# A trunk of convolution, attention and expert layers on one Trainium2 core: the convolution's first chunk, the softmax scaling and the layernorm affine go to other engines, and the layernorm starts two gate tiles sooner

## The chip, the cores and the metric

The kernel runs on one core of one Trainium2 chip. Its engines are TensorE (PE in the profile), VectorE (DVE), ScalarE (ACT), GpSimd (POOL) and SyncE (SP, which here only issues transfers). Each engine runs its own instructions in the order written and waits on semaphores for the others. The metric is the device time of one execution in microseconds (us), as the median of several runs.

## The reference, cut to what matters

The model has two layers (`DEPTH = 2`) over 272 tokens (16 meta tokens and 256 of the input) of width 1024. A layer is a mixer block followed by a block of experts ("peer"). The mixer block projects the normed tokens once and splits the result:

```python
z = h @ w_in
conv_in, c_q, c_kv, k_rope, gate_logits = split(z)
u = conv_in[..., :512] * sigmoid(conv_in[..., 512:])
u = causal_depthwise_conv(u, conv_w, conv_b)           # 31 taps, 512 channels
u = silu(layernorm(u, conv_ln_g, conv_ln_b))           # (u - mu) * rsqrt(var + eps) * g + b
y_conv = u @ w_conv_out
o = chunk_causal_attention(q, k, v)                    # 8 heads, softmax over the keys
y_mla = o @ w_mla_out
merged = sigmoid(gate_logits[..., :1024]) * y_conv + sigmoid(gate_logits[..., 1024:]) * y_mla
x = x + merged @ w_out
```

The expert block scores 16,384 experts per token, picks 16 for each of 8 heads and adds up their outputs. It takes most of the time and is untouched by the change.

## The kernel before, in words

Everything is kept transposed: features on the 128 partitions, tokens along the free dimension. `T` is 272; in the last layer the 16 meta tokens are not needed further on, so the work after the projections runs on `TQ` = 256 columns (`t0` = 16). The schedule is manual: each engine's order is the order in which the Python code emits instructions. Generators (`attention`, `conv2`, `layernorm`) are advanced by `next(...)` between matmul tiles, so that small work of DVE, ACT and POOL falls beside PE's tiles. Weights stream through a ring of four 1 MB buffers (`wraw`), two tiles each, issued by SP.

The part of a layer that the change touches goes so:

- Eight projection tiles for the four chunks of `u` (`ztile`, 8 matmul calls each, two PE instructions a call); DVE and ACT form `u` in `upad`, chunk by chunk.
- **The gate loop**, `for i in range(16)` at line 772: each round is one projection tile on PE (`z`), DVE multiplies it by the token scale into `gt` (line 774), and then `next(att)` and `taps(...)` are called twice. `att` has two steps a round: one puts scores, transposes or the mix with `v` on PE, the other puts the softmax (line 461), its scaling (`scale`, line 478) or copies on ACT and DVE.
- **The convolution** runs meanwhile. Chunks 1 to 3 are 93 taps on DVE (`conv`, line 624), dealt out by the table `TAPS`. Chunk 0 is `conv2`: ACT multiplies the shifted input by a tap's weight (line 631), POOL adds it to `acc` (line 632), tap by tap.
- **The layernorm** (line 679) may begin when all taps are done: PE sums over features (`st`), DVE subtracts the mean, ACT squares, PE sums again (`st2`), DVE makes the reciprocal root in three Newton steps (`rsqrt_steps`, lines 173 to 178), multiplies (702), applies gain and bias (704), ACT takes the sigmoid (706), DVE multiplies by it (710), ACT and DVE split the result into two reduced-precision halves (711, 713) for `uu`.
- **The eight half tiles.** `half_tile(0..3)` multiply the attention output `oo` by `w_mla_out`, `half_tile(4..7)` the convolution's `uu` by `w_conv_out`. Each is 24 matmuls into two PSUM tiles from a pool `z` of three. The weights come as a high half (`high(i)`, ACT, line 653) and a low half (`low(i)`, DVE, line 658). `high(i)` and `low(i)` write buffers that rotate over three places (`wuq`; `seln` and `upad`; `kh` or `acc` and `sqa`). DVE then multiplies the gate in (811) for the first four, or merges (829 to 834) for the last four.
- Eight tiles with `w_out` follow, then the expert block.

`gates(n)` (line 769) lets ACT take the sigmoid of gate tiles in place, two a round, and the rest after the loop. `high(0)`/`low(0)` come in round 14, `high(1)`/`low(1)` after the loop. So before the change the order around the loop's end is set by these lines:

```python
        if i == 14:
            high(0, 1)
            low(0)
    gates(16)
    run_all(att)
    ...
    high(1, 1)
    low(1)
```

## Time and profile before

| What | Value |
|---|---|
| Median of 3 runs (lowest to highest) | 1739.38 us (1739.05 to 1741.44) |
| Profiled execution, its own time | 1741.49 us |
| Its span, first to last instruction | 1739.7 us |
| PE busy, DVE busy, ACT busy, POOL busy | 1706.7, 1157.5, 521.6, 327.1 us |
| Gate loop of the first layer (62 to 147 us): PE, DVE busy | 85.0, 76.5 of 85.0 us |
| End of layernorm and half tiles, first layer (147.0 to 184.1 us): PE, DVE busy | 32.2, 31.5 of 37.1 us |
| The same in the second layer (1023.0 to 1058.85 us): PE busy | 31.0 of 35.85 us |
| POOL's additions for chunk 0, both layers | 60, 51.2 us |
| DVE's taps for chunks 1 to 3, both layers | 180 at lines 624, 90.6 us |

A busy time is the sum of an engine's instruction times; matmuls overlap in the array, so a busy PE says only that it had work. "Idle before" is the gap ahead of an instruction, with the event that ended it. The chain of waits is followed back from the last instruction and shows what set the end.

### The profile page before, as it was taken

The numbers are of one execution on the slowest core, as the hardware profiler recorded it, in microseconds if no ns is written. First come the engines' busy times: TensorE is split into PE (matmuls) and PEld (weight loads), VectorE is DVE, ScalarE is ACT, GpSimd is POOL, SyncE is SP. The second block draws the span as 40 slices with busy tenths as digits, with TensorE's granted clock in tenths as the row PEclk, the third lists the DMA queues.
The fourth block names the chain that finished last, engine by engine and source line by source line (L and its number), as shares of the span: only waits on it lengthen the run. The fifth ranks groups of instructions, "written<-read, shape, count | busy, mean of one in ns | idle before, by whom it ended". The sixth has DMA issues, their size and how long they took to land.

```text
span 1739.7 us, 30197 instructions
## 1 busy us (share of the span) xinstructions
PE 1706.7 (98%) x11867; PEld 1605.3 (92%) x11867; DVE 1157.5 (67%) x2977; ACT 521.6 (30%) x1536; POOL 327.1 (19%) x392
## 2 busy tenths in 40 slices
PE   9999999999999999999999999999999999999998
PEld 7677989989999999999986889899999999999998
DVE  6698678897888544444456987797878885333332
ACT  3444413335544110000024445133355441000000
POOL 0130012222112222322201310112221113122220
PEclk9999999999999999999999999999999999999999
DMA  6223556999999999999962245579999999999995
GB/s 237 98 97 122 194 194 263 372 375 422 420 420 420 421 420 415 421 420 420 418 242 97 98 146 191 197 298 367 396 422 424 423 417 418 393 384 387 400 384 210
DMA packets 80814, 559.42 MB, mean 322 GB/s; under 512 B 9240, under 2 KB 12248, under 8 KB 13208
## 3 DMA queue, kind: packets, MB, share of 16 engines
q1 hardware_dynamic: 49488, 338.54, 49.2%
q0 software_dynamic: 30464, 218.35, 30.9%
q8 instruction: 93, 1.52, 0.3%
q10 hardware_dynamic: 720, 0.60, 0.1%
q14 instruction: 49, 0.40, 0.1%
HBM read 556.18 MB, written 1.05 MB: 320 GB/s over the span
## 4 chain that ended last, share of the span: by engine, by line
PE 65%; DMA 11%; DVE 10%; issue 9%; POOL 3%; ACT 2%; SPq 0%; POOLq 0%; DVEq 0%; ACTq 0%
PE po L56 27%; PE z L56 19%; PE A L56 13%; DMA wraw<-vn 6%; DMA gb<-uv,iww 5%; PE aps L56 3%; POOL gb L1287 2%; DVE va L1298 1%; DVE gb L1312 1%; PE wp L56 1%; PE sc L56 1%; PE xp L56 0%; DVE ex L1011 0%; DVE wuq L658 0%; DVE ex L1008 0%
## 5 line engine op out<-in xcount | busy, mean ns | idle before, releaser
L56 PE MATMUL A<-xh,wraw 128*128 128x160 f32 x3776 | 535.2, 301 | 1.2 <-ACT idxT L925 1.2
L1312 DVE SCALAR_TENSOR_TENSOR gb<-gb,xr 128x1024 f32<-128x1024 f32 x208 | 254.3, 1223 | 406.4 <-DMA gb<-uv,iww 406.0
L56 PEld LDWEIGHTS A<-xh,wraw 128*128 128x128 f32 x3776 | 518.3, 191 | 1.6 <-issue 1.6
L56 PE MATMUL z<-xg,wraw 128*128 128x272 f32 (+2 forms) x1408 | 328.0, 390 | 0.6 <-DMA wraw<-w_in 0.6
L1287 POOL DMA_INDIRECT gb<-uv,iww x208 | 221.6, 1065 | 538.8 <-DVE va L1298 376.2
L56 PEld LDWEIGHTS z<-xg,wraw 128*128 128x128 f32 (+1 forms) x1408 | 258.4, 189 | 54.6 <-issue 8.7
L56 PE MATMUL po<-Xh,wraw 128*128 128x160 f32 x2080 | 287.4, 300 | 3.5 <-DMA wraw<-vn 2.8
L56 PEld LDWEIGHTS po<-Xh,wraw 128*128 128x128 f32 x2080 | 283.2, 190 | 6.6 <-DMA wraw<-vn 5.3
L56 PE MATMUL po<-X,wraw 128*128 128x160 f32 x2016 | 278.4, 301 | 5.3 <-DMA wraw<-vn 2.8
L56 PEld LDWEIGHTS po<-X,wraw 128*128 128x128 f32 x2016 | 275.9, 191 | 7.4 <-DMA wraw<-vn 4.3
L1298 DVE SCALAR_TENSOR_TENSOR va<-gb,am,va 128x1024 f32<-128x1024 f32 x203 | 259.6, 1279 | 1.5 <-ACT am L1323 1.3
L1322 ACT ACTIVATE am<-am 128x1 f32<-128x1 f32 x208 | 41.3, 198 | 595.7 <-DVE gb L1312 595.7
L1226 ACT ACTIVATE ohA<-ohE,wlo 128x128 f16<-128x128 f16 x320 | 105.2, 428 | 6.2 <-DVE ohE L1223 5.5
L632 POOL TENSOR_TENSOR acc<-acc,cp 128x272 f32<-128x272 f32 (+1 forms) x60 | 51.2, 853 | 232.1 <-ACT cp L631 222.8
L1286 POOL COPY warm<-wraw 1x1 f32<-1x1 f32 x86 | 32.8, 382 | 325.1 <-DMA wraw<-vn 324.9
L624 DVE SCALAR_TENSOR_TENSOR acc<-upad,cols,acc 128x272 f32<-128x272 f32 (+1 forms) x180 | 90.6, 556 | 0.2
L1323 ACT ACTIVATE am<-am,iww 128x1 f32<-128x1 f32 x208 | 61.3, 295 | 6.8
L1237 ACT ACTIVATE Xh<-wp 128x260 f32<-128x260 f32 (+18 forms) x80 | 25.0, 313 | 125.1 <-DVE Xh L1234 113.6
L1223 DVE TENSOR_TENSOR ohE<-ioh,idxT 128x512 f16<-128x512 f16 x160 | 60.2, 417 | 0.0
L56 PE MATMUL wp<-ohE,ohA 128*128 128x128 f16 x640 | 51.4, 219 | 0.7 <-DVE ohA L1224 0.7
L56 PEld LDWEIGHTS <-ohA 128*128 128x128 f16 x640 | 43.2, 97 | 5.9 <-DVE ohA L1224 1.3
L56 PE MATMUL A<-xh,we 128*128 128x160 f32 x320 | 45.3, 299 | 0.0
(355 smaller groups left out, 1571.7 us busy)
## 6 DMA issues: line engine op xcount, KB each, us to landing
wraw<-vn SPq DMA_DIRECT2D x128, 1024.0 KB, 10.6
wraw<-u SPq DMA_DIRECT2D x118, 1024.0 KB, 10.1
wraw<-w_in SPq DMA_DIRECT2D x27, 1024.0 KB, 4.8
wraw<-wq SPq DMA_DIRECT2D x16, 1024.0 KB, 4.8
we<-u SPq DMA_DIRECT2D x10, 1024.0 KB, 7.1
wraw<-w_out SPq DMA_DIRECT2D x8, 1024.0 KB, 4.7
wraw<-w_mla SPq DMA_DIRECT2D x4, 1024.0 KB, 4.7
wraw<-w_conv SPq DMA_DIRECT2D x4, 1024.0 KB, 5.1
```

Of the source, the lines that this page charges most:

```text
L56: PE.matmul(o, l, r, start=start, stop=stop, skip_group_check=True)
L624: V.scalar_tensor_tensor(acc[:, c, t0:], u_, weight(c, k), acc[:, c, t0:], op0=OP.mult, op1=OP.add)
L632: G.tensor_tensor(acc[:, 0, t0:], acc[:, 0, t0:], u_[:, t0:], op=OP.add)
L1223: V.tensor_tensor(E[q], ioh[:, None].to_broadcast(full), pairs(q, b), op=OP.is_equal)
L1226: S.activation(A_[1][:, t // 2, :, t % 2], E[0][:, t // 2, :, t % 2], AF.Copy, scale=wlo[:, 4 * b + t:4 * b + t + 1])
L1237: S.activation(x_, p[:, :, a:b].rearrange("p t j -> p j t"), AF.Copy, scale=1.0 / WS)
L1286: G.tensor_copy(warm[0:1], state["w"][0:1, 0:1])
L1287: G.indirect_dma_start(out=g_, out_offset=None, in_=a[f"uv{l}"], in_offset=bass.IndirectOffsetOnAxis(ap=iww[i].bitcast(I32)[:, m // 16, 0, ...
L1298: V.scalar_tensor_tensor(vac[i], r, m_, vac[i], op0=OP.mult, op1=OP.add)
L1312: V.scalar_tensor_tensor(u_, u_, 1.0, xrs[i], op0=OP.mult, op1=OP.mult, accum_out=m_)
L1322: S.activation(m_, m_, AF.Gelu_apprx_tanh)
L1323: S.activation(m_, m_, AF.Copy, scale=iww[i][:, m // 16, 1, m % 16:m % 16 + 1])
```

## The change

Five edits, all in the mixer block of both layers:

1. Chunk 0 of the convolution: ACT makes products of three taps in a tile of three slices (`cp`, two buffers; the first three go to `part`), and one accumulating transfer issued by POOL adds the three slices to `part` inside SBUF. Ten such transfers a layer; the POOL additions are gone. At the end DVE adds the three slices of `part` in two operations. `taps` advances `conv2` three times a round where it was twice.
2. `TAPS` deals the DVE taps out sooner, so that the layernorm is created in round 11, not 13, and its first steps stand in rounds 12 to 15.
3. The softmax scaling (line 484) goes from DVE to ACT.
4. The layernorm's gain and bias go from DVE to ACT: the sigmoid takes them as its scale and bias, and a second activation writes the affine result in place.
5. In `half_tile` the second PSUM tile comes from the pool `aps` (five buffers), not `z`; in the loop over the first four half tiles the layernorm's steps come ahead of `high` and of the gate products.

```diff
--- before.py
+++ after.py
@@ -24,7 +24,7 @@
 EPS = 1e-6
 NEG = -3.0e38
 WS = 16384.0
-TAPS = [2, 2, 5, 5, 6, 6, 6] + [8] * 9
+TAPS = [3, 3, 6, 6] + [8] * 12
 SCALE = 96 ** -0.5
 NC_ = 58
 GROUPS = ((64, 32), (64, 32))
@@ -481,7 +481,7 @@
                 for i in range(2):
                     for e in range(2):
                         x = 2 * i + e
-                        V.tensor_scalar(pr[i][:, e], pr[i][:, e], sm[:, x:x + 1], None, op0=OP.mult)
+                        S.activation(pr[i][:, e], pr[i][:, e], AF.Copy, scale=sm[:, x:x + 1])
 
             def turn(p):
 
@@ -623,14 +623,24 @@
                 else:
                     V.scalar_tensor_tensor(acc[:, c, t0:], u_, weight(c, k), acc[:, c, t0:], op0=OP.mult, op1=OP.add)
 
+        part = mp.tile([128, 3, T], F32, name="part")
+
         def conv2():
 
-            S.activation(acc[:, 0, t0:], upad[:, 0, t0:T], AF.Identity, scale=weight(0, 0), bias=bias(0))
-            for k in range(1, KW):
-                u_ = mp.tile([128, T], F32, name="cp", bufs=4)
-                S.activation(u_[:, t0:], upad[:, 0, k + t0:k + T], AF.Copy, scale=weight(0, k))
-                G.tensor_tensor(acc[:, 0, t0:], acc[:, 0, t0:], u_[:, t0:], op=OP.add)
+            for k in range(0, KW, 3):
+                u_ = mp.tile([128, 3, T], F32, name="cp", bufs=2) if k else part
+                n = min(3, KW - k)
+                for x in range(n):
+                    S.activation(u_[:, x, t0:], upad[:, 0, k + x + t0:k + x + T], AF.Copy if k + x else AF.Identity,
+                                 scale=weight(0, k + x), bias=0.0 if k + x else bias(0))
+                    yield
+                if k:
+                    G.dma_start(part[:, 0:n, t0:], u_[:, 0:n, t0:], accum_op=OP.add)
+            for _ in range(4):
                 yield
+            V.tensor_add(acc[:, 0, t0:], part[:, 0, t0:], part[:, 1, t0:])
+            V.tensor_add(acc[:, 0, t0:], acc[:, 0, t0:], part[:, 2, t0:])
+            yield
 
         parts = {}
 
@@ -671,7 +681,7 @@
             next_w()
             ps = []
             for f in range(2):
-                p = zp.tile([128, 512], F32, name="z", bufs=3)[:, :TQ]
+                p = (aps() if f else zp.tile([128, 512], F32, name="z", bufs=3))[:, :TQ]
                 three(i, p, (src[:, 0], src[:, 1]), 4 * f, range(4), 0, 3)
                 ps.append(p)
             return ps
@@ -701,9 +711,9 @@
             for c in range(4):
                 V.tensor_mul(acc[:, c, t0:], acc[:, c, t0:], rl)
             for c in range(4):
-                V.tensor_scalar(acc[:, c, t0:], acc[:, c, t0:], cl[:, C_LG + c:C_LG + c + 1],
-                                cl[:, C_LB + c:C_LB + c + 1], op0=OP.mult, op1=OP.add)
-                S.activation(sg[:, c, :TQ], acc[:, c, t0:], AF.Sigmoid)
+                g_, b_ = cl[:, C_LG + c:C_LG + c + 1], cl[:, C_LB + c:C_LB + c + 1]
+                S.activation(sg[:, c, :TQ], acc[:, c, t0:], AF.Sigmoid, scale=g_, bias=b_)
+                S.activation(acc[:, c, t0:], acc[:, c, t0:], AF.Identity, scale=g_, bias=b_)
             yield
             yield
             for c in range(4):
@@ -773,16 +783,17 @@
             z = ztile(t0)
             V.tensor_mul(gt[i // 8][:, i % 8, t0:], z, rs[:, t0:])
             if ln is None:
-                more = next(att, "end")
-                taps(TAPS[i] // 2, 1)
+                next(att, None)
+                taps(TAPS[i] // 2, 2)
                 next(att, None)
                 taps(TAPS[i] - TAPS[i] // 2, 1)
-                if more == "end" and min(ck.values()) == KW and next(cvp, "end") == "end":
-                    run_all(cvp)
+                if min(ck.values()) == KW and next(cvp, "end") == "end":
                     ln = layernorm()
             else:
                 next(ln, None)
+                next(att, None)
                 next(ln, None)
+                next(att, None)
             if "exp" in vt:
                 gates(min(i + 1, ng[0] + 2))
             if i == 14:
@@ -805,14 +816,14 @@
         low(1)
         for i in range(4):
             ps = half_tile(i, oo)
+            next(ln, None)
+            next(ln, None)
             if i < 3:
                 high(i + 2, 1)
             for f in range(2):
                 V.tensor_mul(gt[1][:, 2 * i + f, t0:], gt[1][:, 2 * i + f, t0:], ps[f])
             if i < 3:
                 low(i + 2)
-            next(ln, None)
-            next(ln, None)
         run_all(ln)
         high(5, 1)
         low(5)
```

What this does to the order at the loop's end, first layer. ACT from the square of the layernorm on (`wuq`, `seln` and `kh` are the high halves of half tiles 0, 1 and 2, `g_607` and `g_596` the second eight gate tiles, `sqa` the sigmoid's result), before:

```order
L769 ACTIVATE g_607<-g_607 128x272 x2
L653 ACTIVATE wuq<-wraw 128x1024
L769 ACTIVATE g_607<-g_607 128x272 x6
L653 ACTIVATE seln<-wraw 128x1024
L653 ACTIVATE kh<-wraw 128x1024
L653 ACTIVATE wuq<-wraw 128x1024
L706 ACTIVATE sqa<-acc 128x272 x4
L653 ACTIVATE seln<-wraw 128x1024
L711 ACTIVATE uk<-acc 128x272 x4
```

and after, up to the first of four pairs of lines 715 and 716 (one pair a chunk):

```order
L699 ACTIVATE sqa<-acc 128x272 x4
L779 ACTIVATE g_595<-g_595 128x272 x4
L779 ACTIVATE g_596<-g_596 128x272 x2
L663 ACTIVATE wuq<-wraw 128x1024
L715 ACTIVATE sqa<-acc,cols_61 128x272
L716 ACTIVATE acc<-acc,cols_61 128x272
```

The first layernorm square (699) and these pairs have moved ahead of most of the gate sigmoids. Still on ACT, behind the fourth pair:

```order
L779 ACTIVATE g_596<-g_596 128x272 x6
L663 ACTIVATE seln<-wraw 128x1024
L721 ACTIVATE uk<-acc 128x272 x4
L663 ACTIVATE kh<-wraw 128x1024
L663 ACTIVATE wuq<-wraw 128x1024
```

The layernorm's activations, which stood behind four high halves, now stand ahead of `seln` (half tile 1), and the six last gate sigmoids with them.

DVE at the same place (`wuq`, `upad`, `kh` are the low halves of half tiles 0, 1, 2; the operation on `z` at line 774 or 784 is the gate product of a projection tile), before:

```order
L658 TENSOR_TENSOR wuq<-wraw,wuq 128x1024
L774 TENSOR_TENSOR g_607<-z,rq_ym 128x272
L695 TENSOR_SCALAR rq_x<-aps 128x272
L173 TENSOR_SCALAR rq_w<-rq_x 128x272
L174 TENSOR_SCALAR rq_yl<-rq_w 128x272
L176 SCALAR_TENSOR_TENSOR rq_w<-rq_yl 128x272
L177 TENSOR_TENSOR rq_w<-rq_w,rq_x 128x272
L178 SCALAR_TENSOR_TENSOR rq_yl<-rq_w,rq_yl 128x272
L658 TENSOR_TENSOR upad<-wraw,seln 128x1024
L811 TENSOR_TENSOR g_607<-g_607,z 128x272 x2
L658 TENSOR_TENSOR kh<-wraw,kh 128x1024
```

and after:

```order
L178 SCALAR_TENSOR_TENSOR rq_yl<-rq_w,rq_yl 128x272
L668 TENSOR_TENSOR wuq<-wraw,wuq 128x1024
L784 TENSOR_TENSOR g_596<-z,rq_ym 128x272
L712 TENSOR_TENSOR acc<-acc,rq_yl 128x272 x4
L668 TENSOR_TENSOR upad<-wraw,seln 128x1024
L720 TENSOR_TENSOR acc<-acc,sqa 128x272 x4
L723 TENSOR_TENSOR uk<-acc,uk 128x272 x4
L824 TENSOR_TENSOR g_596<-g_596,z 128x272
L824 TENSOR_TENSOR g_596<-g_596,aps 128x272
L668 TENSOR_TENSOR kh<-wraw,kh 128x1024
```

All three Newton steps and the product with the root now stand ahead of half tile 1's low half, and the rest of the layernorm stands between the low halves of half tiles 1 and 2.

## The prediction

> **What bounds the kernel now.** I read the page's busy times first, then stretches around the mixer block's stages, then the chain of waits, and last each engine in order of time.
>
> ```profile
> PE 1706.7 (98%) x11867; PEld 1605.3 (92%) x11867; DVE 1157.5 (67%) x2977; ACT 521.6 (30%) x1536; POOL 327.1 (19%) x392
> ```
>
> ```profile
> 62.00:147.00 85.00, 85.00 (x463) 66.63 (x462) 76.52 (x191) 33.49 (x92) 24.73 (x28) 1.00 0.31 110
> 147.00:184.10 37.10, 32.18 (x212) 28.89 (x211) 31.49 (x66) 18.84 (x34) 0.00 (x0) 1.00 0.40 147
> 1023.00:1058.85 35.85, 31.00 (x211) 28.67 (x210) 0.95 0.41 150
> ```
>
> PE has work for 98% of the span: a change can win only where PE stands idle. In a stretch's row stand its length, then the busy time of PE, its weight load, DVE, ACT and POOL, then PE's granted clock (the row of the second layer has PE and weight load alone). Through the gate loop (62 to 147 us) PE is never idle, though DVE is busy for 76.5 of 85 us. **So whatever only makes DVE's load lighter in the loop (no scaling, no POOL beside it) is worth nothing by itself.** PE's idle time within reach is 37.10 - 32.18 = 4.9 us in the first layer and 35.85 - 31.00 = 4.85 in the second, around the half tiles. The chain of waits has a piece there (start, length, engine, tile) that shows the pattern, a high half on ACT, a low half on DVE; then PE in order of time:
>
> ```profile
> 167.65 1.05 ACT seln L653
> 168.70 0.02 issue
> 168.72 1.23 DVE upad L658
> ```
>
> ```profile
> 135.73 11.27 PE L56 MATMUL z<-xg,wraw 128*128 128x272 f32 x48
> 146.83 2.00 PE L56 MATMUL aps<-acc,ones 128*128 128x272 f32 x8
> 148.67 3.83 PE L56 MATMUL z<-xg,wraw 128*128 128x272 f32 x16
> 152.33 2.00 PE L56 MATMUL aps<-sqa,ones 128*128 128x272 f32 x8
> 153.97 3.47 PE L56 MATMUL z<-sq,wuq 128*128 128x272 f32 x24
> 157.27 0.29 PE L56 MATMUL z<-sq,seln 128*128 128x272 f32 x1
> 158.21 0.40 PE L56 MATMUL z<-sq,upad 128*128 128x272 f32 x1 [0.65 <-DVE upad L658]
> 161.21 1.68 PE L56 MATMUL z<-sq,kh 128*128 128x272 f32 x12
> 185.71 0.29 PE L56 MATMUL z<-xh,acc 128*128 128x272 f32 x1
> ```
>
> Half tile 0 starts at 153.97, the work behind half tile 7 at 185.71: 31.7 us. One half tile takes 157.27 - 153.97 = 3.30, or, its first matmul apart, 161.21 - 158.21 = 3.00 for 23, so 3.13 for 24. Eight would take 25.0 to 26.4: the stage loses 5.3 to 6.7 us.
>
> **The change, part by part.** From 135.73 on PE has four projection tiles and the layernorm's two sums before half tile 0, in both kernels; only the order among them changes. With PE never idle before, half tile 0 can start at 153.97 again. Three tiles take 146.83 - 135.73 = 11.1, one 3.7. Round 15's tile is now the last thing ahead of 153.97, so round 14's is ready at 153.97 - 3.7 = 150.3.
>
> *DVE.* The second Newton step is queued behind the gate product of round 14, which waits for that tile.
>
> ```profile
> 159.90 0.43 DVE L176 SCALAR_TENSOR_TENSOR rq_w<-rq_yl 128x272 f32<-128x272 f32 x1
> 162.63 0.78 DVE L811 TENSOR_TENSOR g<-g,z 128x272 f32<-128x272 f32 x2
> 163.33 1.22 DVE L658 TENSOR_TENSOR wuq<-wraw,wuq 128x1024 fp32r<-128x1024 f32 x1
> 164.46 1.49 DVE L702 TENSOR_TENSOR acc<-acc,rq_yl 128x272 f32<-128x272 f32 x4
> 176.17 0.43 DVE L829 TENSOR_TENSOR az<-g,z 128x272 f32<-128x272 f32 x1
> 179.89 0.43 DVE L829 TENSOR_TENSOR az<-g,z 128x272 f32<-128x272 f32 x1
> ```
>
> A gate product takes 0.35 (two in 163.33 - 162.63), two Newton steps 162.63 - 159.90 = 2.73, a low half 1.13 until the next may start (164.46 - 163.33) and 1.22 until its result. So: 150.3 + 0.35 + 2.73 = 153.4 low half 0 starts, ready at 154.6; round 15's gate product and the first product with the root (0.43) end at 153.4 + 1.13 + 0.35 + 0.43 = 155.3. Half tile 0 waits 0.6 us for its low half and ends at 154.6 + 3.0 = 157.6.
>
> *ACT* then has eight activations with scale and bias per partition, the in-place one of each pair waiting for its partner, then six gate sigmoids, and only then the high half of half tile 1 (`seln`).
>
> ```profile
> 152.87 2.17 ACT L769 ACTIVATE g<-g 128x272 f32<-128x272 f32 x6
> 154.94 1.05 ACT L653 ACTIVATE seln<-wraw 128x1024 fp32r<-128x1024 f32 x1
> 192.21 0.51 ACT L186 ACTIVATE xg<-hT,cols 128x272 f32<-128x272 f32 x1
> 192.62 0.41 ACT L190 ACTIVATE sq<-hT 128x272 f32<-128x272 f32 x1
> 703.22 0.20 ACT L1322 ACTIVATE am<-am 128x1 f32<-128x1 f32 x1 [4.43 <-DVE gb L1312]
> 703.45 0.29 ACT L1323 ACTIVATE am<-am,iww 128x1 f32<-128x1 f32 x1
> ```
>
> A scaled activation of this shape takes 0.51 and lets the next start after 0.41 (192.62 - 192.21); one that waits for the activation ahead of it starts 0.03 after that one's end (703.45 against 703.42). A pair is 0.51 + 0.03 + 0.41 = 0.95. The trace has no sigmoid with scale and bias. Plain ones come every 0.35 (six in 2.07), so a pair is at least 0.70; with both waiting it is at most 1.08. I take 0.95, from the row with the nearest operands. Four pairs 3.8, six sigmoids 154.94 - 152.87 = 2.07, `seln` 1.05, low half 1 on DVE 1.22: 155.3 + 8.1 = 163.5 with the hand-overs (0.02 each). **Half tile 1 has both halves at 163.5, and PE is free from 157.6: it waits 5.9 us in one piece.** Before, half tile 1 ran from 158.2.
>
> Behind that low half DVE has the product with the sigmoid (4 x 0.35), the split (4 x 0.35), the gate products of half tile 0 (0.7) and low half 2 (1.22): 163.5 + 4.7 = 168.2 for half tile 2. From there the layernorm is through. DVE has two gate products and a low half for each half tile (0.7 + 1.13), later a merge and a low half (179.89 - 176.17 = 3.7, three times, against PE's 3.1 to 3.3, entered more than a tile ahead), and ACT a high half and two copies. PE runs on: 168.2 + 6 x 3.13 (or 3.30) - 0.1 = 186.9 to 187.9, against 185.71: 1.2 to 2.2 us later. **I take 1.6.**
>
> The second layer has the same order at 256 columns.
>
> ```profile
> 1029.27 3.45 PE L56 MATMUL z<-sq,wuq 128*128 128x256 f32 x24
> 1053.79 3.10 PE L56 MATMUL z<-uk,wuq 128*128 128x256 f32 x24
> 1056.73 0.28 PE L56 MATMUL z<-uk,seln 128*128 128x256 f32 x1
> 1060.38 0.28 PE L56 MATMUL z<-xh,acc 128*128 128x256 f32 x1
> ```
>
> In the first layer half tile 2 starts 168.2 - 153.97 = 14.2 behind half tile 0; with operations 256/272 as long on the way I take 14.0. A clean half tile is 1056.73 - 1053.79 = 2.94: 1029.27 + 14.0 + 6 x 2.94 - 0.1 = 1060.8, against 1060.38: **0.4 later** (with 3.3 a half tile 2.6).
>
> *PE's clock.* The second layer's gaps already cost clock before the change:
>
> ```profile
> 1042.00:1046.00 4.00, 1.80 (x13) 1.59 (x14) 3.23 (x9) 2.37 (x6) 0.00 (x0) 1.00 0.43 182
> 1046.90:1050.40 3.50, 3.50 (x18) 3.50 (x19) 3.04 (x7) 2.00 (x2) 0.00 (x0) 0.52 0.00 0
> ```
>
> PE was busy for 1.8 of 4 us, and the next 3.5 us ran at a granted clock of 0.52. That loss is inside the 1060.38 above. The gap of 5.9 us should do the same, now in both layers: half tile 1 takes about 4.7 instead of 3.0 us, from 163.5 to 168.2, when half tile 2 gets its low half at the earliest. So most of it is hidden: I charge **0.3 a layer**. If the low clock outlasts half tile 1, it costs up to 1.7 a layer (3.5 us at half).
>
> The Trainium skill (TensorE: Matmul & The Clock Gate, Part 1: The HAM clock gate) says that the array falls to half clock after an idle window of about 3.4 us and returns after a busy one, and that the windows run free of the work. The 0.52 for 3.5 us agrees; the fall after a stretch that was busy 1.8 of 4 us does not need a wholly idle window. By that rule alone the old gaps would have cost nothing and the new one a window's half, 1.7 a layer, 1744.8.
>
> *Taps and transfers* lie beside PE's tiles.
>
> ```profile
> 69.99 2.54 DVE L624 SCALAR_TENSOR_TENSOR acc<-upad,cols,acc 128x272 f32<-128x272 f32 x6
> 131.00 4.42 DVE L624 SCALAR_TENSOR_TENSOR acc<-upad,cols,acc 128x272 f32<-128x272 f32 x8
> 119.82 3.83 PE L56 MATMUL z<-xg,wraw 128*128 128x272 f32 x16
> 130.49 3.93 PE L56 MATMUL z<-xg,wraw 128*128 128x272 f32 x16
> ```
>
> ```profile
> wraw<-w_in SPq DMA_DIRECT2D x27, 1024.0 KB, 4.8
> mv<-svm POOLq DMA_DIRECT2D x4, 4.0 KB, 3.8
> ```
>
> Eight taps beside POOL's additions take 4.42; without, 2.54 x 8/6 = 3.4. Two rounds of the loop are 130.49 - 119.82 = 10.7 on PE, one 5.3; DVE's new round is 3.4 + 0.35 and about 1 us of attention. So eight taps a round fit, and the last one ends before the first sum is due at 135.73 + 3.7 = 139.4. An accumulating transfer is 128 x 3 x 272 x 4 bytes = 408 KB. A plain one lands in 3.8 (4 KB from POOL) to 4.8 us (1 MB); that the destination is read as well could double it, 9.6. Each waits for the one before and one is due a round, so they pile up from 5.3 us on. I take 4.5, nearest the plain rows: no cost. ACT gets some 7 us of scaling a layer into 85 - 33.5 = 51.5 us of idle time, and the softmax's scaled rows are wanted two rounds later. The second PSUM pool only removes waits that the sums above no longer hold.
>
> **Sum.** 1.6 + 0.4 + 2 x 0.3 = 2.6 us on the profiled execution's span of 1739.7 (its own time is 1741.49, near the top of the runs shown). I set the sum on the median: 1739.4 + 2.6 = 1742.0.
>
> **Rivals.** (a) *The clock stays low past half tile 1*: 1.7 instead of 0.3 a layer, or two such windows: 1745 to 1748. For it: the fall after shorter gaps. Against it: that fall lasted 3.5 us, hardly more than the half tile it would hit.
>
> (b) *The layernorm's move pays.* If half tile 1 is not held up, the stage loses only the 0.6, not 5.3 to 6.7, and the second layer keeps its clock: 5 us a layer, 1729. Every us off the gap is one a layer; below a gap of about 2.9 the time passes under 1735.9. Against it: ACT works in order, and the 8.1 us between 155.3 and 163.5 are rows; the lowest pair (0.70) brings 1 us a layer, 1740.
>
> (c) *The accumulating transfers are late.* DVE then stands at its first addition of `part` at the end of round 9, with the gate products and soon PE's tiles behind it. At 7 us each the ten end 10 x (7 - 5.3) = 17 us late; DVE's slack from there to 139.4 is about 14 us of PE's rounds less 7 of its own work. So PE loses some 10 a layer, 1760. Against it: the plain rows; for it: no row of an accumulating one. The Trainium skill (SBUF — State Buffer, Who interferes with whom) says that DVE can keep POOL off a shared port and so delay its descriptors; the slow taps beside POOL show that the two share something, no run here shows a late descriptor.
>
> **Chances.** The forecast 0.55, with its own range 1739 to 1744; (a) 0.22; (b) 0.13; (c) 0.10. A measurement of this kernel tells a change of 0.2%, 3.5 us, from none: 1735.9 to 1742.9. Slower: (c) 0.10, most of (a) 0.18, the forecast's upper end 0.08, in all 0.36. Faster: (b) 0.12. Same: 0.52. The range leaves out (b)'s 1729 and (c): 1738 to 1749.
>
> **What would show it.** Right: PE idle 5 to 6 us ahead of half tile 1's first matmul on `upad`, released by line 668; about 0.6 ahead of half tile 0's second; next to none from half tile 2 on; a granted clock near 0.5 for some 3.5 us behind the gap; taps at 0.42; transfers landing in under 5 us. Wrong: a gap under 3 us there (b); gaps in the gate loop or DVE waiting at line 641 (c); a low clock in half tile 2 (a).

## The result: 0.8% slower, and the profile after

| | Before | After |
|---|---|---|
| Median of the runs timed together (5 each) | 1740.43 us | 1753.88 us (1751.76 to 1759.54) |
| Ratio, 95% interval | | 1.0078 [1.0061, 1.0095] |
| Profiled execution: its time, its span | 1741.49, 1739.7 us | 1754.29, 1752.5 us |

The forecast was 1742.0 us with a range of 1738 to 1749. The kernel came out 13.4 us slower than before, 5 us above the range.

The first rows are the page's busy times of the changed kernel; the second fence has three stretches of it (length, then busy PE, weight load, DVE, ACT, POOL, granted clock, DMA share, GB/s): the first layer's gate loop, its half tiles, and a piece of the second layer's gate loop.

```profile
PE 1712.1 (98%) x11867; PEld 1607.8 (92%) x11867; DVE 1126.6 (64%) x2941; ACT 541.1 (31%) x1576; POOL 320.1 (18%) x352
```

```profile
62.00:147.00 85.00, 85.00 (x464) 66.60 (x462) 64.47 (x184) 43.61 (x116) 8.89 (x10) 1.00 0.56 149
147.00:184.10 37.10, 30.53 (x199) 28.43 (x198) 26.51 (x54) 17.67 (x30) 0.00 (x0) 0.91 0.41 144
975.00:1000.00 25.00, 22.23 (x106) 17.82 (x105) 15.15 (x43) 14.98 (x44) 5.02 (x4) 0.86 0.67 142
```

The third of these stretches in the kernel before:

```profile
975.00:1000.00 25.00, 25.00 (x144) 20.46 (x142) 24.59 (x62) 14.63 (x45) 8.19 (x11) 1.00 0.24 85
```

In the first layer DVE is 12 us lighter in the gate loop and PE as full as before, which brings nothing; the half tiles have lost 1.65 us of PE's busy time and part of its clock. Both were forecast. The second layer's gate loop was not: PE, never idle there before, stands for 2.8 of 25 us, and the mean granted clock of the stretch is 0.86. Cutting the two profiled executions at the same places tells what each stage took (us; "to half tile 0" runs from the layer's first projection tile, in the first layer from the span's start; "half tiles" from the first matmul of half tile 0 to the first behind half tile 7):

| Stage | Before | After | Difference |
|---|---|---|---|
| Layer 1, to half tile 0 | 153.97 | 153.44 | -0.5 |
| Layer 1, half tiles | 31.74 | 33.61 | +1.9 |
| Layer 2, to half tile 0 | 140.45 | 146.34 | **+5.9** |
| Layer 2, half tiles | 31.11 | 33.40 | +2.3 |
| All else (eight tiles with `w_out`, expert blocks, the end) | 1382.4 | 1385.7 | +3.3 |

The last row is mostly the expert blocks, in which no edit lies. Over the fourteen kernels of this text the first layer's block took 673.6 to 678.1 us between the same two places (675.2 before, 676.5 after), in no order that follows an edit. So of these 3.3 us I explain nothing and take them as scatter.

**First layer, half tiles.** PE in order of time (start, length, idle time ahead and what ended it), and ACT:

```profile
153.44 0.49 PE L56 MATMUL z<-sq,wuq 128*128 128x272 f32 x1
154.63 1.66 PE L56 MATMUL z<-sq,wuq 128*128 128x272 f32 x11 [0.69 <-DVE wuq L668]
163.00 0.59 PE L56 MATMUL z<-sq,seln 128*128 128x272 f32 x1 [5.21 <-ACT seln L663]
164.26 0.59 PE L56 MATMUL z<-sq,upad 128*128 128x272 f32 x1 [0.67 <-DVE upad L668]
168.69 1.88 PE L56 MATMUL z<-sq,kh 128*128 128x272 f32 x12
187.05 0.29 PE L56 MATMUL z<-xh,acc 128*128 128x272 f32 x1
```

```profile
155.36 0.62 ACT L715 ACTIVATE sqa<-acc,cols 128x272 f32<-128x272 f32 x1 [9.04 <-DVE acc L712]
156.01 0.62 ACT L716 ACTIVATE acc<-acc,cols 128x272 f32<-128x272 f32 x1
156.53 0.60 ACT L715 ACTIVATE sqa<-acc,cols 128x272 f32<-128x272 f32 x1
160.00 2.01 ACT L779 ACTIVATE g<-g 128x272 f32<-128x272 f32 x6
161.91 1.04 ACT L663 ACTIVATE seln<-wraw 128x1024 fp32r<-128x1024 f32 x1
```

The picture is the forecast one: a single gap ahead of half tile 1 (5.21 us for its high half, 0.67 more for its low half), the pairs and six gates ahead of `seln` on ACT, no gap from half tile 2 on, and the work behind half tile 7 at 187.05 against a forecast of 186.9 to 187.9. Only the pairs are longer than forecast: four take 160.00 - 155.36 = 4.64, one 1.16.

**Second layer, gate loop.** PE, ACT and POOL of the changed kernel (POOL with two rows of the first layer ahead):

```profile
978.25 3.62 PE L56 MATMUL z<-xg,wraw 128*128 128x256 f32 x16
981.71 1.60 PE L56 MATMUL aps<-kh,xh 98*128 98x144 f32 x8
986.08 2.04 PE L56 MATMUL aps<-t,vt 128*64 128x256 f32 x12 [2.77 <-ACT t L504]
988.05 6.41 PE L56 MATMUL z<-xg,wraw 128*128 128x256 f32 x16
```

```profile
979.35 0.91 ACT L634 ACTIVATE cp<-upad,cols 128x256 f32<-128x256 f32 x2 [4.11 <-DMA part<-cp]
984.64 0.91 ACT L634 ACTIVATE cp<-upad,cols 128x256 f32<-128x256 f32 x2 [1.96 <-DMA part<-cp]
985.45 0.57 ACT L504 ACTIVATE t<-aps 128x512 f32<-128x512 f32 x1
```

```profile
86.47 0.86 POOL L638 DMA_DIRECT2D part<-cp  x1 [7.11 <-ACT cp L634]
90.99 0.86 POOL L638 DMA_DIRECT2D part<-cp  x1 [3.66 <-DMA part<-cp]
...
957.31 1.41 POOL L638 DMA_DIRECT2D part<-cp  x1 [87.05 <-ACT cp L634]
962.54 1.29 POOL L638 DMA_DIRECT2D part<-cp  x1 [3.82 <-DMA part<-cp]
972.95 1.26 POOL L638 DMA_DIRECT2D part<-cp  x1 [9.12 <-DMA part<-cp]
979.80 1.25 POOL L638 DMA_DIRECT2D part<-cp  x1 [5.59 <-DMA part<-cp]
985.09 1.25 POOL L638 DMA_DIRECT2D part<-cp  x1 [4.04 <-DMA part<-cp]
...
1012.62 0.90 POOL L638 DMA_DIRECT2D part<-cp  x1 [3.99 <-DMA part<-cp]
```

Read from below. POOL issues a transfer when the one ahead has landed. In the first layer that takes 4.5 us here (90.99 - 86.47; 4.5 to 5.1 where one waits for the one ahead, once 6.4); in the second these rows are 5.2, 10.4, 6.9 and 5.3 us apart, and over all ten the mean is (1012.62 - 957.31) / 9 = 6.15 us. ACT wants to write products into one of two buffers, has to stand until a transfer has freed it (4.11, then 1.96 us), and only behind that come the copies `t` at 985.45. PE, which mixes with `t`, stands 2.77 us, and its next projection tile takes 6.41 us instead of 3.62, at a granted clock of 0.58 (988.0 to 994.5 us). The gap and the slow tile together are 5.6 of the stage's 5.9 us.

### The profile page after: what moved, and what is told of

It reads as the page before. It is cut to its first block, busy times and chain, and to the rows that moved or that the text cites. A ratio compares the mean times of both kernels' runs of the same rounds, so it can differ in the third digit from the quotient of the medians.

```text
span 1752.5 us, 30137 instructions
## 1 busy us (share of the span) xinstructions
PE 1712.1 (98%) x11867; PEld 1607.8 (92%) x11867; DVE 1126.6 (64%) x2941; ACT 541.1 (31%) x1576; POOL 320.1 (18%) x352
## 3 DMA queue, kind: packets, MB, share of 16 engines
q0 software_dynamic: 35648, 225.92, 33.4%
## 4 chain that ended last, share of the span: by engine, by line
PE 64%; DMA 15%; issue 8%; DVE 8%; ACT 2%; POOL 2%; POOLq 0%; SPq 0%; DVEq 0%; ACTq 0%
PE po L56 24%; PE z L56 18%; PE A L56 15%; DMA wraw<-vn 8%; DMA gb<-uv,iww 5%; PE aps L56 4%; POOL gb L1298 2%; DMA part<-cp 1%; PE wp L56 1%; DVE gb L1323 1%; DVE va L1309 1%; PE sc L56 1%; DMA wraw<-u 1%; PE xp L56 0%; DVE upad L668 0%
## 5 line engine op out<-in xcount | busy, mean ns | idle before, releaser
L1298 POOL DMA_INDIRECT gb<-uv,iww x208 | 233.7, 1124 | 521.0 <-DVE va L1309 375.3
L1297 POOL COPY warm<-wraw 1x1 f32<-1x1 f32 x86 | 43.8, 509 | 317.7 <-DMA wraw<-vn 317.6
L624 DVE SCALAR_TENSOR_TENSOR acc<-upad,cols,acc 128x272 f32<-128x272 f32 (+1 forms) x180 | 76.8, 486 | 0.2
L638 POOL DMA_DIRECT2D part<-cp x20 | 21.3, 1065 | 246.3 <-ACT cp L634 176.1
L1103 POOL TENSOR_TENSOR xh<-xg,rq_ym 128x272 f32<-128x272 f32 (+1 forms) x16 | 11.3, 739 | 199.9 <-DVE sv L906 102.4
```

The source lines that it names most:

```text
L624: V.scalar_tensor_tensor(acc[:, c, t0:], u_, weight(c, k), acc[:, c, t0:], op0=OP.mult, op1=OP.add)
L638: G.dma_start(part[:, 0:n, t0:], u_[:, 0:n, t0:], accum_op=OP.add)
L1297: G.tensor_copy(warm[0:1], state["w"][0:1, 0:1])
L1298: G.indirect_dma_start(out=g_, out_offset=None, in_=a[f"uv{l}"], in_offset=bass.IndirectOffsetOnAxis(ap=iww[i].bitcast(I32)[:, m // 16, 0, ...
```

## The experiments

Two causes are to be told apart and sized: the transfers in the second layer, and ACT's queue ahead of half tile 1. Each kernel is the changed one with the edit shown, unless another is named. The kernel before was timed beside each; its median was 1741.2 to 1741.7 us in the three groups of experiments. The half tiles' length is given as layer 1 / layer 2.

| Kernel | Median, us | Ratio to before, 95% | Layer 2 to half tile 0 | Half tiles |
|---|---|---|---|---|
| before | 1740.43 | 1 | 140.45 | 31.74 / 31.11 |
| after | 1753.88 | 1.0078 [1.0061, 1.0095] | 146.34 | 33.61 / 33.40 |
| taps side by side | 1745.67 | 1.0020 [1.0011, 1.0029] | 140.20 | 33.59 / 32.35 |
| side by side, three buffers | 1745.09 | 1.0019 [1.0010, 1.0028] | 140.18 | 33.83 / 33.03 |
| plain transfers | 1745.53 | 1.0025 [1.0016, 1.0035] | 140.18 | 33.59 / 32.32 |
| three buffers, sums in three runs as in the change | 1763.18 | 1.0123 [1.0104, 1.0142] | 155.53 | 34.74 / 33.43 |
| additions on GpSimd | 1748.59 | 1.0035 [1.0022, 1.0047] | 140.19 | 33.59 / 32.97 |
| half tile 1 sooner | 1752.87 | 1.0059 [1.0047, 1.0072] | 146.08 | 33.57 / 31.36 |
| side by side, softmax scaling on DVE | 1744.51 | 1.0017 [1.0008, 1.0026] | 140.18 | 33.57 / 32.31 |
| side by side, affine on DVE | 1742.52 | 1.0007 [0.9998, 1.0017] | 140.18 | 32.56 / 30.48 |
| side by side, halves sooner, gates spread | 1739.68 | 0.9993 [0.9984, 1.0002] | 140.18 | 30.63 / 29.33 |
| the same, affine on DVE | **1731.64** | **0.9946 [0.9933, 0.9960]** | 140.17 | 27.17 / 26.15 |
| the same, additions on GpSimd | 1736.31 | 0.9977 [0.9962, 0.9992] | 140.21 | 27.07 / 27.34 |
| before, in that order | 1742.02 | 1.0005 [0.9996, 1.0014] | 140.42 | 31.73 / 31.13 |

### The taps side by side

In the second layer the three slices of a group are 272 columns long, of which 256 are moved: three runs of 1024 bytes a partition. This kernel packs them into one of 3072.

```diff
-        part = mp.tile([128, 3, T], F32, name="part")
+        def three_taps(name, bufs=1):
+            t_ = mp.tile([128, 3 * T], F32, name=name, bufs=bufs)
+            return t_[:, 0:3 * TQ].rearrange("p (x t) -> p x t", x=3)
+        part = three_taps("part")
...
-                u_ = mp.tile([128, 3, T], F32, name="cp", bufs=2) if k else part
+                u_ = three_taps("cp", 2) if k else part
```

> The changed kernel with the three taps side by side alone: one run of 3072 bytes a partition in the second layer, two buffers as in the change. If the three runs a partition make the second layer's transfers slow (4.8 to 6.4 us, one of 10, against 4.5 us for one run in the first layer), they fall to about 4.5 us, ScalarE's waits at line 634 shrink to under 1 us each and 3 to 6 us come back: 1748 to 1751 us. If it is the weights' traffic beside them that makes them slow, the waits stay and the time is 1753 to 1755 us.

It took 1745.67 us, 8.2 below the change and lower than I had expected. POOL again:

```profile
969.65 0.85 POOL L642 DMA_DIRECT2D part<-cp  x1 [6.99 <-ACT cp L638]
974.09 0.86 POOL L642 DMA_DIRECT2D part<-cp  x1 [3.58 <-DMA part<-cp]
979.31 0.85 POOL L642 DMA_DIRECT2D part<-cp  x1 [4.37 <-DMA part<-cp]
```

Where one waits for the one ahead, transfers now start 4.4 to 5.2 us apart (5.31 in the mean over all ten), an issue takes 0.86 instead of 1.26, some issues wait for ACT's products and not for a landing, and the stage up to half tile 0 is back at 140.20: the gap in PE's gate loop is gone, though ACT still stands up to 3.5 us at a group. The same bytes in one run instead of three are worth the whole 5.9 us. The second layer's half tiles are 1 us shorter as well, but that does not follow the transfers: over the seven kernels with the same code there they take 32.3 to 33.4 us.

### A third buffer, with and without the packing

The first edit is on top of the taps side by side:

```diff
-            t_ = mp.tile([128, 3 * T], F32, name=name, bufs=bufs)
-            return t_[:, 0:3 * TQ].rearrange("p (x t) -> p x t", x=3)
+            t_ = mp.tile([128, 3 * TQ], F32, name=name, bufs=bufs)
+            return t_.rearrange("p (x t) -> p x t", x=3)
...
-                u_ = three_taps("cp", 2) if k else part
+                u_ = three_taps("cp", 3 if t0 else 2) if k else part
```

> The changed kernel, with two edits to the accumulating transfers: the three taps lie side by side (in the second layer one run of 3072 bytes a partition instead of three of 1024), and in the second layer there are three buffers of products instead of two. Theory W (ScalarE, in order, stands at the first tap of a group until the transfer of two groups back has landed, and TensorE then misses the copies t that stand behind it): with a third buffer a transfer has two rounds of some 3.7 us; the waits of ScalarE at line 634 in the second layer (3.87, 2.78, 4.11, 1.96 us) go, TensorE's busy time between the gate tiles is unbroken again, the stage up to st is some 6 us shorter, and the kernel takes 1747 to 1749 us. Rival S (the softmax scaling that was put on ScalarE makes the copies t late): no change, 1752 to 1755. Rival Q (the transfers' queue itself is too slow, over 5 us each whatever the buffers): the wait stays at the last groups and moves to VectorE's addition of the parts; 1750 to 1753.

1745.09 us, below all three expectations: packing and a third buffer together gain no more than packing alone, so with the packing done a third buffer adds nothing. So I gave the change three buffers and left its sums in three runs (the products lie side by side here):

```diff
-                u_ = mp.tile([128, 3, T], F32, name="cp", bufs=2) if k else part
+                u_ = part[:, :, t0:] if not k else mp.tile([128, 3, TQ], F32, name="cp", bufs=3 if t0 else 2)
...
-                    G.dma_start(part[:, 0:n, t0:], u_[:, 0:n, t0:], accum_op=OP.add)
+                    G.dma_start(part[:, 0:n, t0:], u_[:, 0:n], accum_op=OP.add)
```

> The changed kernel with three buffers of products in the second layer, and the sums still in three runs of 1024 bytes a partition. In the profile of the change a transfer is issued only when the one ahead has landed, 5.1 to 6.9 us apart (10.4 once), so a third buffer lends one transfer of slack but no pace. If the buffers were the cause: 1745 to 1747 us. If the pace of the transfers is: ScalarE's waits come one group later and the time is 1748 to 1753 us.

1763.18 us, outside both expectations: worse than two buffers by 9 us. VectorE shows why:

```profile
1012.42 1.66 DVE L624 SCALAR_TENSOR_TENSOR acc<-upad,cols,acc 128x256 f32<-128x256 f32 x4
1025.19 0.43 DVE L641 TENSOR_TENSOR acc<-part 128x256 f32<-128x256 f32 x1 [11.11 <-DMA part<-cp]
```

With a third buffer the transfers are no faster (6.72 us apart in the mean, 6.15 in the change); what is new is that DVE, in order, stands 11.1 us at its first addition of `part`, with the gate products and the layernorm behind it. The two buffers were not the cause. They only decided who waits: ACT a little in every group, or DVE for all of it at the end. The pace of the transfers is the cause.

### Plain transfers

```diff
-                    G.dma_start(part[:, 0:n, t0:], u_[:, 0:n, t0:], accum_op=OP.add)
+                    G.dma_start(part[:, 0:n, t0:], u_[:, 0:n, t0:])
```

> The changed kernel with plain transfers in place of the accumulating ones: each overwrites the sums, so the first chunk's sum over taps is left out; bytes, runs, buffers and waits are the same. If adding in the transfer is what it costs, the second layer's transfers fall from some 5.2 us between issues to 3 to 4 us, ScalarE's waits go, and the kernel takes 1745 to 1748 us. If the runs of 1024 bytes are, plain or not, the transfers stay at 5 us and the time at 1752 to 1755 us.

1745.53 us, as the first of the two has it. This kernel leaves out the first chunk's sum over taps. POOL, where a transfer waited for the landing of the one ahead:

```profile
958.98 0.81 POOL L638 DMA_DIRECT2D part<-cp  x1 [87.33 <-ACT cp L634]
962.88 0.78 POOL L638 DMA_DIRECT2D part<-cp  x1 [3.10 <-DMA part<-cp]
```

3.9 us, in three runs a partition (3.5 in two other places, once 5.7). In the first layer of the same kernel, where a partition's bytes are one run of 3264, it is no different, 3.9 and here 3.3:

```profile
119.74 0.54 POOL L638 DMA_DIRECT2D part<-cp  x1 [6.70 <-ACT cp L634]
123.08 0.54 POOL L638 DMA_DIRECT2D part<-cp  x1 [2.80 <-DMA part<-cp]
```

So the runs cost where the transfer adds, and hardly where it copies: it is the adding and the runs together. The queue of these transfers from 940 to 1030 us (packets, MB, share of the 16 engines), in the change, with the taps side by side, and plain:

```profile
q0 software_dynamic: 3744, 3.67, 27.6%
```

```profile
q0 software_dynamic: 1440, 3.67, 22.6%
```

```profile
q0 software_dynamic: 1056, 3.67, 10.9%
```

The same 3.67 MB goes as 3744 packets when added in short runs, as 1440 when added in long ones, as 1056 when only copied. Adding doubles the time that the engines spend (22.6 against 10.9%); short runs put a fifth on top (27.6 against 22.6%).

### The additions on GpSimd

```diff
-        part = mp.tile([128, 3, T], F32, name="part")
...
+            S.activation(acc[:, 0, t0:], upad[:, 0, t0:T], AF.Identity, scale=weight(0, 0), bias=bias(0))
+            for k in range(1, KW):
+                yield
+                u_ = mp.tile([128, T], F32, name="cp", bufs=4)
+                S.activation(u_[:, t0:], upad[:, 0, k + t0:k + T], AF.Copy, scale=weight(0, k))
+                G.tensor_tensor(acc[:, 0, t0:], acc[:, 0, t0:], u_[:, t0:], op=OP.add)
```

> The changed kernel with the first chunk's taps added on GpSimd as before the change (a product on ScalarE, an addition of 0.82 us on GpSimd, four buffers), at the change's own pace of three taps a round and with all else of it. Theory W: without transfers ScalarE never stands at a tap, since three additions take 2.5 us of a 3.7 us round; the second layer's gate loop is unbroken, 6 to 7 us come back: 1746 to 1748 us. If the scaling on ScalarE or three taps a round are the cause, the gap stays: 1752 to 1755 us.

1748.59 us, 0.6 above what I had expected. The second layer's loop is whole again, but the median is 3 us above the packed transfers (the two intervals just overlap), and the first layer lost 1.7 us in its gate loop, at a place where the kernels with transfers have gaps of 0 to 0.9 us:

```profile
109.62 0.35 PE L553 MATMUL aps<-ident,sm__731 16*16 16x16 f32 x8 [1.70 <-ACT pr L474]
```

DVE and POOL just before (ACT's softmax waits for DVE's maxima behind these taps):

```profile
100.09 3.17 DVE L624 SCALAR_TENSOR_TENSOR acc<-upad,cols,acc 128x272 f32<-128x272 f32 x4
```

```profile
99.57 2.98 POOL L633 TENSOR_TENSOR acc<-acc,cp 128x272 f32<-128x272 f32 x3 [4.76 <-ACT cp L632]
```

Four taps take 3.2 us beside POOL's additions and 1.7 alone. The same in the fastest order, further down, cost 4.7 us, of which 1.7 are a gap at this place again. So the transfers are worth something at three taps a round, once they are packed: they keep POOL off DVE. The group of the 180 taps (busy time, mean ns) in the kernel before, in the change, and in the fastest order with additions on GpSimd:

```profile
L624 DVE SCALAR_TENSOR_TENSOR acc<-upad,cols,acc 128x272 f32<-128x272 f32 (+1 forms) x180 | 90.6, 556 | 0.2
```

```profile
L624 DVE SCALAR_TENSOR_TENSOR acc<-upad,cols,acc 128x272 f32<-128x272 f32 (+1 forms) x180 | 76.8, 486 | 0.2
```

```profile
L624 DVE SCALAR_TENSOR_TENSOR acc<-upad,cols,acc 128x272 f32<-128x272 f32 (+1 forms) x180 | 97.0, 595 | 0.2
```

The Trainium skill (SBUF — State Buffer, Who interferes with whom) says that a VectorE instruction with two SBUF inputs contends with a GpSimd instruction that reads SBUF. By that rule the taps lose beside additions and not beside transfers; the traces agree, 3.2 against 1.7 us for four.

### The softmax scaling

```diff
-                        S.activation(pr[i][:, e], pr[i][:, e], AF.Copy, scale=sm[:, x:x + 1])
+                        V.tensor_scalar(pr[i][:, e], pr[i][:, e], sm[:, x:x + 1], None, op0=OP.mult)
```

(with the taps side by side)

> The changed kernel with the taps side by side, and the softmax's scaling on VectorE as before the change. With the transfers no longer in the way neither engine is full in the gate loop (ScalarE 37.9 and VectorE 36.6 of the 45 us from 955 to 1000, with the taps side by side): no change, 1744.5 to 1747 us. Rival S (ScalarE's four scalings a pair make its copies t late for TensorE): 1742 to 1744 us.

1744.51 us against 1745.67, intervals of the ratios [1.0008, 1.0026] and [1.0011, 1.0029]: no difference that can be told, and the stages of the table are the same to 0.04 us. Which engine scales is of no account here, with the taps packed.

### Half tile 1's halves ahead of the layernorm's last steps

```diff
             else:
+                if i == 15:
+                    high(1, 1)
+                    low(1)
                 next(ln, None)
...
-        high(1, 1)
-        low(1)
```

> The changed kernel with the two halves of half tile 1 (lines 663 and 668) made in round 15 ahead of the layernorm's last steps, not behind them. Theory H (what is left of the layernorm's move is spent because half tile 1 waits for its halves behind eight activations and six gates): TensorE's 5.2 us ahead of half tile 1 in the first layer and 5.5 us in the second go, and the low clock behind them; the layernorm is late by about 1.5 us instead, which half tile 4 does not notice as it starts some 20 us on. Each layer gains 5 to 7 us: 1740 to 1744 us. Rival L (the chain of the layernorm through DVE and ScalarE sets when half tile 4 can start): the gap moves to half tile 2 or 4, and under 2 us a layer come back: 1750 to 1753 us.

1752.87 us, not to be told from the change by the two intervals (the transfers are as in the change), and 9 us above what theory H expected. PE in the first layer:

```profile
165.36 0.59 PE L56 MATMUL z<-sq,kh 128*128 128x272 f32 x1 [4.59 <-ACT kh L663]
166.82 2.86 PE L56 MATMUL z<-sq,kh 128*128 128x272 f32 x11 [0.87 <-DVE kh L668]
```

The gap has moved on by one half tile: now half tile 2's copy stands behind the same eight activations and six gates, and behind the four copies of `u` (line 721). Rival L gave the right time, but not for its reason. Half tile 4, which needs the layernorm's result, shows no gap; ACT's queue holds the copies.

### The affine step on VectorE

```diff
-                S.activation(sg[:, c, :TQ], acc[:, c, t0:], AF.Sigmoid, scale=g_, bias=b_)
-                S.activation(acc[:, c, t0:], acc[:, c, t0:], AF.Identity, scale=g_, bias=b_)
+                V.tensor_scalar(acc[:, c, t0:], acc[:, c, t0:], g_, b_, op0=OP.mult, op1=OP.add)
+                S.activation(sg[:, c, :TQ], acc[:, c, t0:], AF.Sigmoid)
```

(with the taps side by side, all else of the change)

> The changed kernel with the taps side by side, and the layernorm's affine step on VectorE with a plain sigmoid on ScalarE behind it, as before the change; the layernorm still starts two gate tiles sooner. Theory A (ScalarE's eight activations of some 0.6 us, then six gates, hold back the first copy of half tile 1): ScalarE's part shrinks from 4.6 us (four pairs of 1.16) to four sigmoids paced by VectorE (0.44 each), so the copy comes some 2 us sooner, the gap ahead of half tile 1 falls from 5.2 to about 3 us, with less of the low clock, and the kernel takes 1740 to 1743 us against 1745.7 with the taps side by side alone. If the gap hangs on VectorE's part of the layernorm, nothing changes: 1744.5 to 1747 us.

```profile
161.09 0.47 PE L56 MATMUL z<-sq,seln 128*128 128x272 f32 x1 [3.27 <-ACT seln L667]
```

1742.52 us: 3.2 below the taps side by side, for 1.9 us less of gap in the first layer and 2.2 in the second (the half tiles are 1.0 and 1.9 us shorter). Theory A holds, with its number.

### Both halves sooner, gates two a half tile, and then the affine step too

```diff
             else:
+                if i == 15:
+                    high(1, 1)
+                    low(1)
+                    high(2, 2)
+                    low(2)
                 next(ln, None)
...
-        gates(16)
+        gates(10)
...
-            if i < 3:
+            if 0 < i < 3:
                 high(i + 2, 1)
+            gates(min(16, 12 + 2 * i))
```

> The changed kernel with the taps side by side, the halves of half tiles 1 and 2 made in round 15 ahead of the layernorm's last steps, and the last six gates issued two a half tile; the affine step stays on ScalarE. Moving the halves of half tile 1 alone has only moved the gap to half tile 2, whose copy stood behind eight activations, six gates and four copies of u. Theory A: with both halves in the 9 us in which ScalarE idles and the gates out of the way, TensorE runs through half tiles 0 to 2; half tile 3 may wait 1 to 2 us; half tile 4 needs u, which is ready by then. Per layer 4 to 6 us of idle time and low clock go: 1734 to 1739 us. If the layernorm's chain to u sets the end whatever stands ahead of it, the gap sits at half tile 4 and the time is 1743 to 1746 us.

1739.68 us, level with the kernel before and 0.7 us above what I expected. What is left in the first layer is half tile 3, whose copy still stands behind the pairs, and a low clock behind it (eleven matmuls in 2.27 us, not 1.66):

```profile
165.46 0.36 PE L56 MATMUL z<-sq,wuq 128*128 128x272 f32 x1 [1.51 <-ACT wuq L667]
167.55 2.27 PE L56 MATMUL z<-sq,wuq 128*128 128x272 f32 x11 [1.73 <-DVE wuq L672]
```

With the affine step on VectorE as above:

> The same as the kernel with the halves and the gates moved, with the affine step on VectorE and a plain sigmoid on ScalarE as well. Theory A: half tile 3's copy is then not late either, 1 to 2 us a layer less than with the affine step on ScalarE, 1731 to 1737 us: faster than the kernel before by 0.3 to 0.5 per cent. If ScalarE's activations were hidden behind half tiles 0 to 2, it equals the kernel with the affine step on ScalarE within 1 us.

1731.64 us, 0.54% faster than the kernel before. In the first layer one gap is left behind half tile 0, and the clock is full behind it:

```profile
165.85 1.66 PE L56 MATMUL z<-sq,wuq 128*128 128x272 f32 x11 [1.52 <-DVE wuq L672]
```

The affine step alone had brought 3.2 us, the order alone 6.0; together they bring 14.0, not 9.1. PE's waits within the first layer's half tiles do add up: 6.6 us with the taps side by side, 1.8 less with the affine step on DVE, 2.6 less with the order, 4.4 less with both. What goes beyond the sum there is the clock: from 155 to 190 us it is 0.90 with either gap of over 3 us ahead of half tile 1, 0.95 with the two of 1.5 and 1.7, and 1.00 with one of 1.5.

### The same with additions on GpSimd, and the order alone

> The fastest kernel so far (taps side by side, halves sooner, gates two a half tile, affine step on VectorE) with the first chunk's additions on GpSimd at three taps a round, as before the change, in place of the accumulating transfers. If the transfers only carry the pace of three taps and are worth nothing by themselves, it takes 1730 to 1734 us. Additions on GpSimd in place of the transfers at the change's own order came out at 1748.6 against 1745.7 us, 3 us that nothing explains yet; if they are real it takes 1734 to 1736 us.

1736.31 us, 0.3 above the upper of the two ranges. The half tiles are as short in the first layer (27.07), but they start at 157.04 instead of 153.79: PE stands 1.73 us at the place named above, and its next projection tile takes 5.62 us instead of 3.93, at a granted clock of 0.72 (109 to 115 us; 1.00 with the transfers). The second layer's took 1.2 us more. PE there, at half tile 3, with additions and with transfers:

```profile
1038.88 2.25 PE L56 MATMUL z<-sq,wuq 128*128 128x256 f32 x11 [1.67 <-DVE wuq L660]
```

```profile
1035.99 1.55 PE L56 MATMUL z<-sq,wuq 128*128 128x256 f32 x11 [1.66 <-DVE wuq L672]
```

The gap is the same, but with the additions the clock behind it is 0.59 (1038.8 to 1042.5 us) and with the transfers 1.00. So the additions cost the first layer's gap, 1.7 us, in both orders; the other 3 us of the 4.7 are a low clock behind gaps that elsewhere left it up. Why it fell here and not there the runs do not show.

The last kernel is the one before the change, with nothing but the copies of half tile 2 beside those of half tile 1 and the gates spread:

```diff
-        gates(16)
+        gates(10)
...
         high(1, 1)
         low(1)
+        high(2, 2)
+        low(2)
...
-            if i < 3:
+            if 0 < i < 3:
                 high(i + 2, 1)
+            gates(min(16, 12 + 2 * i))
```

> The kernel before, with the two orders that made the changed one fast and with nothing else of the change: the halves of half tile 2 made together with those of half tile 1 behind round 15, and the last six gates issued two a half tile. Theory M (the layernorm's two tiles are worth their 3 to 4 us a layer once ScalarE's queue is clear of gates): here u is still ready only at 172, so half tile 4 waits as before and at most the 1 to 2 us of stalls at half tiles 1 and 2 go: 1737 to 1741 us, against 1731.6 for the changed kernel in that order. Rival O (the order alone is the gain, the layernorm's start is worth nothing): 1731 to 1734 us.

1742.02 us, no different from before, and 1 us above what I had expected at most. Half tile 4 still waits for the layernorm's result, at the same place as before:

```profile
170.74 0.39 PE L56 MATMUL z<-uk,seln 128*128 128x272 f32 x1 [1.36 <-ACT uk L711]
```

Nor did the stalls ahead of it go: half tile 1 stands 0.65 us for its low half and half tile 3 1.26 us for a gate product, as before. So this order by itself, with the copies behind round 15, is worth nothing. The rest of the change in its own order is no faster than before either (1742.52 us with the taps side by side and the affine step on VectorE). Together they shorten the first layer's half tiles from 31.7 to 27.2 us, and with the additions on GpSimd to 27.1, so the transfers have no part in that. That it is the layernorm's earlier start which the order needs is argued and not shown: no kernel has that start without the second PSUM pool, none has that pool alone, and the gap of 1.26 us for a gate product is in no kernel with the pool.

## Why the prediction was wrong, point by point

**The failed step is "taps and transfers".** It took 4.5 us for a transfer and wrote "no cost". Three things in it were off.

- The 4.5 us hold for the first layer (4.5 to 5.1, once 6.4), with one run of 3264 bytes a partition. The second layer was not worked out. There the tile keeps its 272 columns and moves 256, in three runs, and a transfer follows the one ahead by 5.1 to 10.4 us. What that cost, 5.9 us, is about half the gap it made for PE (2.77) and half the low clock behind the gap (6.41 us for a tile, not 3.62).
- The step itself named the point from which transfers pile up, 5.3 us. The packed ones, 5.31 apart in the mean, just keep that pace; those of the change, 6.15 apart, end 9 x 0.84 = 7.6 us late by it, and the loop lost 5.9. The threshold was good for the second layer, the price was not. (In the first the issues are 5.71 us apart in the mean, a third of them waiting for ACT's products, and PE has no gap: there the rounds with attention are longer than the late ones from which the 5.3 was read.)
- It never named the two buffers. Rival (c) let the delay build up until DVE stands at line 641, for 1760 us. That is what three buffers gave, 11.1 us at that line and 1763, though by 15 us in the second layer and not by some 10 in each, so the match of the totals is luck. With two, ACT stands in most groups instead, the softmax and the copies `t` stand behind it, and PE stands for these. I had counted what ACT adds (7 us into 51 us of idle time) and not asked what it waits for and what is queued behind that wait.

**The half tiles, first layer: right in mechanism and total, the total in part by luck.** 1.6 plus 0.3 for the clock was forecast, +1.9 measured, and most rows came near where they were put. The one mis-sized term is the pair of activations: 0.95 forecast, 1.16 measured (above the upper bound of 1.08), since a sigmoid or identity with scale *and* bias from a column takes 0.60 to 0.62, while the row I took it from has one such operand and takes 0.51. Half tile 1's low half came at 164.26 instead of 163.5. Half tile 0 had started 0.5 us sooner, and half tile 2 then followed in 4.4 us and not 4.7. From half tile 0 to half tile 2 it took 15.25 us where 14.2 was forecast, and the six half tiles behind it 18.4 where 18.7 to 19.7 was: that the end came where it was put is in part luck. The Trainium skill (ScalarE: Activation LUTs, What ACT_TABLE_LOAD costs) has an activation at 186 ns plus 0.833 ns a column plus 93 ns for each operand that is a column; an estimate from it for 272 columns and two operands is 599 ns, and the trace agrees.

**The half tiles, second layer: too small.** 0.4 plus 0.3 was forecast, +2.3 measured in the change, and +1.2 to +2.3 over the seven kernels with the same code there. Its gap is as long as the first layer's:

```profile
1047.68 0.58 PE L56 MATMUL z<-sq,seln 128*128 128x256 f32 x1 [5.47 <-ACT seln L663]
```

I had scaled the first layer's working down to 256 columns where the gap did not shrink: half tile 2 starts 16.0 us behind half tile 0 (1054.01 - 1038.06), not 14.0, and the six behind it take the 17.5 that were forecast. The rest of the spread is the clock: with the taps side by side half tile 1 takes 4.1 us from its first matmul on `upad`, in the change 5.1 (0.50 from 1047.7 to 1053.5 us). To that extent rival (a) came true, at 0.5 to 1.6 us and not at the 3 to 6 of its price.

**The clock** fell where it was said, behind the gap (0.50 from 163.5 to 167.0 us in the first layer), and half tile 2 started at 168.69 against a forecast of 168.2.

**Taps worth nothing by themselves: right as far as the runs go.** 13.8 us of DVE's time were saved over both layers, and the first layer's gate loop, 12 us lighter on DVE, is no shorter for it. No kernel makes the taps lighter and nothing else; and at three taps a round the additions on GpSimd cost a gap of 1.7 us, so there a lighter load is worth that.

**Rival (b)** had the price of the gap right: 1729 if half tile 1 is not held up. With the copies out from behind ACT's pairs and gates, and the transfers packed, 1731.64 was measured: its 5 us a layer were 4.6 and 5.0 in the half tiles. The change could have been faster than before by 0.5%; its order and its affine step on ACT and its strided tile cost 22 us.

## What to carry to other kernels

A tile that is cut shorter in one stage turns one run a partition into several; cost a transfer per shape of its runs, above all one that adds, and compare it with the round in which its buffer is wanted back. Where a new wait goes on an in-order engine, name what stands behind it before counting that engine's idle time: here the copies that TensorE needed. And work that is moved ahead of a stall pays only when the queue it is moved into is clear of work that nobody awaits yet; here neither the change nor the order gained anything alone.

## What the runs showed of the hardware that I had not expected

- A transfer from SBUF to SBUF that adds is slower than a copy of the same 384 KB, and by more in shorter runs. Between issues that wait for the one ahead: plain in runs of 1024 bytes 3.5 to 3.9 us (once 5.7), in one run of 3264 (408 KB) 3.3 to 3.9; added in runs of 3072 4.4 to 5.2, added in runs of 1024 5.1 to 7.0 (once 10.4, and once 9.4 in the kernel with three buffers). Packets of the queue: 1056 plain and 3744 added in runs of 1024, 1440 added in runs of 3072. What made the one of 10.4 is not settled.
- The issue on POOL grows with both: 0.54 us plain in one run, 0.75 plain in three, 0.86 added in one, 1.26 added in three.
- What a gap of PE costs is not its length alone. Behind the gaps of over 3 us listed above the clock fell, to 0.50 behind the two of 5.2 and 5.5 us; behind single gaps of 1.7 us it stayed at 1.00 (the fastest kernel, second layer) or fell to 0.59 and 0.72 (the same with additions on GpSimd). Before the change and with only the order changed, the first layer's half tiles have nearly the same gaps, and the clock from 155 to 190 us is 1.00 in one and 0.95 in the other.
